# The 32x32 diagonal inverses of a chunked gated DeltaNet: a tile of their own, stored by transfers straight into block-diagonal tiles

## The chip, the cores and the metric

The kernel runs on one core of a Trainium2 chip. The metric is the device time of one execution in microseconds (us). All engines of the core run side by side, each through its own list of instructions in order: TensorE (PE, matmuls; PEld is its weight load), VectorE (DVE), ScalarE (ACT), GpSimd (POOL), and SyncE (SP), whose queue issues the transfers (DMAs).

## What is computed

The reference is a two-layer decoder step over 1024 prompt tokens and 8 x 4 sample tokens, model width 1024, in float32. Layer 0 is sliding-window attention, layer 1 a gated DeltaNet with 8 query/key heads and 16 value heads of width 128. The change touches only the chunked solve of layer 1's prompt part:

```python
lower = jnp.where(strict, jnp.einsum('nbhik,nbhjk->nbhij', kb, kc) * decay, 0.0)
rhs = jnp.concatenate([vc * bc[..., None], kb * jnp.exp(gc)[..., None]], axis=-1)
sol = lax.linalg.triangular_solve(lower + jnp.eye(chunk), rhs,
                                  left_side=True, lower=True, unit_diagonal=True)
...
def step(S, xs):
    u = w_v_c - jnp.einsum('bhck,bhkv->bhcv', w_k_c, S)
    o = jnp.einsum('bhck,bhkv->bhcv', q_dec_c, S) + jnp.einsum('bhij,bhjv->bhiv', qk_c, u)
    S = S * g_tot_c[..., None, None] + jnp.einsum('bhck,bhcv->bhkv', k_dec_c, u)
```

The kernel uses chunks of 128 tokens. It inverts each 128x128 unit triangular matrix: first its four 32x32 diagonal blocks, then the blocks beside them by matmuls.

## The kernel before

Layer 1 works on eight pairs r = 0 to 7, each one query/key head with its two value heads (`hq` in the code). A pair has 8 chunks times 2 heads = 16 triangular matrices, so 64 diagonal blocks. Beside this PE computes the large input projections of the layer (`ps_pj` in the profile; `project`, L548), 24 matmuls for each group of tokens. Each pair goes through these stages, each a Python generator that gives way wherever it says `yield`:

- `solve` (L1832): products k.kT on PE into PSUM, multiplied on DVE into the four tiles `UZ`; the diagonal 32x32 blocks go by 16 transfers to a DRAM tile `Ld`.
- `invert` (L1882): the 64 blocks come back as `X` (64 partitions, one block each, 32 x 32 in the free dimensions). POOL writes ones on the diagonal and zeros the diagonal blocks of `UZ`. Then DVE does 31 elimination steps of two instructions each (`tmp<-X`, `X<-X,tmp`). The block is stored as its transpose, so `X` holds the input above the diagonal and collects the inverse below it, in the same tile. `X` goes to DRAM (`Xdd`) and comes back as `Xc` (four transfers).
- `diagonal` (L1914), four times a pair: POOL multiplies `Xc` by a triangular mask, which drops the input still above the diagonal, into one of two block-diagonal tiles `Xd` (four instructions, 128 a kernel). PE multiplies `UZ` with `Xd`, ACT copies the product negated to `M`, DVE transposes `Xd`'s blocks into `UZ`.
- `blocks` (L1936): six rounds (v = 0 to 5) of small matmuls `ps_lg<-UZ,M`, each followed by DVE copies into `UZ`.
- `decayed` (L1961): products q.kT in two PSUM banks, 16 DVE instructions `DP<-ps_lg,sj,DP`, eight for each bank.
- `chain` (L1984): the recurrence over the 8 chunks. Each step starts with `ps_ob<-vo,UZ` on PE and goes PE, DVE, PE, DVE. It starts when round v = 2 of `blocks` is written.

**What sets the order of the work.** The program's order on each engine is fixed when the kernel is built. `Core` (L96) keeps modelled times of each engine. While PE's projections are written out one after another, `stages` (L496) goes through the list of waiting generators by rank and lets each run until a condition of its own fails, such as `idle("vector")` (the modelled DVE is free) or `soon(X)` (modelled data is nearly there). The ranks stand in the table `KR` (L242): for pair 1, `invert` has 10, `decayed` 35; for pair 0, `blocks` has 10. Two rules matter here. The PSUM banks `lg`, two of them, are handed out strictly in turn: `bank` (L535) waits until the bank used two requests ago was given back. And the projection of `kT` for pair r + 1 is not written out before chain r - 1 is finished (`until(lambda: finished[0] >= r - 1)`, L2171); so for r = 1 all projections stop until the chain of pair 0 is done.

The pool `gs` (opened at L1613 in `decays`, right side of SBUF) holds `X`, `tmp`, `Xc`, `Xd` and `M`; the pool `kwp` (L1319, left side) holds the split weights of the first `kT` projection until the end.

Of the kernel before, what the change touches and what calls it, by code (L numbers as in the profile page):

```python
# [5 lines left out]
F32 = mybir.dt.float32  # L6
# [3 lines left out]
ALU = mybir.AluOpType  # L10
# [4 lines left out]
P = 128  # L15
# [204 lines left out]
def body(tc, I, O, cst_ap, dbg=None):  # L220
    nc = tc.nc
    from contextlib import ExitStack, nullcontext
    es = ExitStack()
# [71 lines left out]
    C = {k: cst[:, o:o + w] for k, (o, w) in COFF.items() if o < nkeep}  # L295
# [189 lines left out]
    def weave(gen, name, hq=None):  # L485

        rank = KR[hq][name] if hq is not None else K[name]
        i = 0
        while i < len(jobs) and jobs[i][3] <= rank:
            i += 1  # L490
        jobs.insert(i, [lambda: True, gen, name, rank])
# [25 lines left out]
    def plain():  # L517
        return not isinstance(nc, Core)
# [4 lines left out]
    def soon(*ts):  # L523
        return lambda: plain() or nc.ready(ts) <= nc.free["tensor"] + AH
# [237 lines left out]
    if True:  # L762
# [469 lines left out]
        for t in range(NB + 1):  # L1232
            parts = P if t < NB else TS
            pv = psb("pj3")[0:parts, 0:256]
            n = 0
# [51 lines left out]
        nc = Core(tc)  # L1287
# [23 lines left out]
    if True:  # L1311
# [4 lines left out]
        hp = es.enter_context(tc.tile_pool(name="hp2", bufs=1, side="left"))  # L1316
        h2hi, h2lo = ([hp.tile([P, KD, b - a], F32R, tag=f"{nm}{i}", name=nm) for i, (a, b) in enumerate(GRP)]
                      for nm in ("h2hi", "h2lo"))
        kwp = es.enter_context(tc.tile_pool(name="kwp", bufs=1, side="left"))  # L1319
        x2_guard = tc.tile_pool(name="x2", bufs=1, side="left")  # L1320
        x2 = Watched(nc, x2_guard.__enter__(), since=nc.free["tensor"])
        nc.parts.add(x1d.tensor.name)
# [2 lines left out]
        kwr, kw = [], []  # L1325
# [110 lines left out]
        for i, t in enumerate(turned_):  # L1436
# [7 lines left out]
            for kk, hf in order if i < NB else sorted(order, key=lambda o: o[::-1]):  # L1444
                if True:
                    ns = slice(hf * 512, (hf + 1) * 512)
                    if hf not in pjs:
                        tag = ("pj", "pj", "mi", "mi")[outs[0] % 4]
# [50 lines left out]
    gs, Xd, gs_guard = None, [], None  # L1499

    def decays():
# [22 lines left out]
        for gi, (a, b) in enumerate(GRP):  # L1524
# [3 lines left out]
            n = 0  # L1528
# [81 lines left out]
        nc.vector.tensor_copy(gbs[:, 1, :], bt[:, :, NB])  # L1610
        ab2_guard.__exit__(None, None, None)
        ab_guard.__exit__(None, None, None)
        gs_guard = tc.tile_pool(name="gs", bufs=1, side="right")  # L1613
        gs = Watched(nc, gs_guard.__enter__(), since=nc.free["tensor"] + SL)
        for i in range(2):
            Xd.append(gs.tile([P, 4, P], F32, name=f"Xd{i}"))
            nc.gpsimd.memset(Xd[i], 0.0)
        weave(decay_blocks(0, states[0]), "decay")
        weave(solve(0, states[0]), "solve", 0)
        weave(decayed(0, states[0]), "decayed", 0)  # L1620
# [22 lines left out]
    if True:  # L1643
# [75 lines left out]
        def proj_kq(hq, st, which=(0, 1), run=None):  # L1719
            for nm, ct, s0 in [(("kT", HQ + hq, HQ), ("qT", hq, 0))[w] for w in which]:  # L1720
                full = gp.tile([P, T], F32, tag=nm, name=nm, bufs=2)
                st[nm] = full
                conv(ct, s0 + hq, lambda gi, a0, b0, full=full: full[:, a0:b0],
                     lambda gi, *a, nm=nm: st.update({nm + "done": gi == 2}), run)
            return st
# [81 lines left out]
        def spare(hq):  # L1807

            return "mi" if hq == 0 else "lg"
# [72 lines left out]
        def invert(hq, st, Ld, Xdd):  # L1882
            UZ, lg = st["UZ"], spare(hq)
            yield lambda: inverted[0] == hq


            X = gs.tile([64, 32, 32], F32, tag="X", name="X")
            tmp = gs.tile([64, 256], F32, tag="tmp", name="tmp")
            nc.sync.dma_start(X, Ld)
            yield soon(X)  # L1890
            nc.gpsimd.memset(X.rearrange("p i c -> p (i c)")[:, 0:1024:33], 1.0)
            for cp_ in range(4):
                uv = UZ[cp_].rearrange("p h c i -> p (h c) i")
                for b in range(4):
                    bs = slice(32 * b, 32 * b + 32)
                    nc.gpsimd.memset(uv[bs, :, bs], 0.0)
            yield soon(X)
            for k in range(31):
                n, m = 31 - k, k + 1
                tv = tmp[:, 0:n * m].rearrange("p (i c) -> p i c", c=m)  # L1900
                yield idle("vector")
                nc.vector.tensor_tensor(tv, X[:, k, k + 1:].unsqueeze(2).to_broadcast([64, n, m]),
                                        X[:, k, 0:m].unsqueeze(1).to_broadcast([64, n, m]), ALU.mult)
                nc.vector.tensor_tensor(X[:, k + 1:, 0:m], X[:, k + 1:, 0:m], tv, ALU.subtract)
            nc.sync.dma_start(Xdd, X)
            inverted[0] += 1
            yield lambda: solved[0] == hq
            Xc = gs.tile([P, 16, 32], F32, tag="Xc", name="Xc")
            for b in range(4):
                nc.sync.dma_start(Xc[32 * b:32 * b + 32], Xdd[16 * b:16 * b + 16].rearrange("q i c -> i q c"))  # L1910

            lg, Ms, uzs = "lg", [], [t_.rearrange("p h c i -> p (h c) i") for t_ in UZ]

            def diagonal():  # L1914

                for cp_, uz in enumerate(uzs):
                    xd = Xd[cp_ % 2]
                    yield soon(Xc)
                    for b in range(4):
                        bs = slice(32 * b, 32 * b + 32)  # L1920
                        nc.gpsimd.tensor_tensor(xd[bs, :, bs], Xc[bs, 4 * cp_:4 * cp_ + 4, :],
                                                C["lo32"][bs, :].unsqueeze(1).to_broadcast([32, 4, 32]), ALU.mult)
                    yield lambda: st.get("pairs", 0) >= cp_ - 2
                    yield ready(xd)
                    pm = yield from bank(lg)
                    pmv = pm.rearrange("p (q i) -> p q i", q=4)
                    for q in range(4):
                        nc.tensor.matmul(pmv[:, q, 0:96], uz[:, q, :], xd[:, q, 0:96], start=True, stop=True)
                    yield soon(pm)
                    M = gs.tile([P, 4, 96], F32, tag="M", name="M", bufs=3)  # L1930
                    nc.scalar.activation(M, pmv[:, :, 0:96], AF.Copy, scale=-1.0)
                    give(lg, pm)
                    nc.vector.transpose(uz.rearrange("p q i -> p (q i)"), xd.rearrange("p q i -> p (q i)"))
                    Ms.append(M)

            def blocks():  # L1936


                for v in range(6):
                    parts = [(v - s, 64 - 32 * s) for s in range(3) if 0 <= v - s < 4]  # L1940
                    yield lambda: len(Ms) > parts[0][0]
                    yield ready(*[Ms[cp_] for cp_, _ in parts], *[UZ[cp_] for cp_, _ in parts])
                    pz = yield from bank(lg)
                    pzv = pz.rearrange("p (q i) -> p q i", q=4)
                    for q in range(4):
                        for cp_, r0 in reversed(parts):
                            rs, cs = slice(r0, r0 + 32), slice(r0 + 32, P)
                            nc.tensor.matmul(pzv[rs, q, cs], Ms[cp_][:, q, rs], uzs[cp_][:, q, cs], start=True, stop=True,
                                             skip_group_check=True)
                    yield soon(pz)  # L1950
                    for cp_, r0 in reversed(parts):
                        rs, cs = slice(r0, r0 + 32), slice(r0 + 32, P)
                        nc.vector.tensor_copy(uzs[cp_][rs, :, cs], pzv[rs, :, cs])
                    give(lg, pz)
                    st["pairs"] = max(0, v - 1)
                solved[0] += 1

            weave(blocks(), "blocks", hq)
            weave(diagonal(), "blocks", hq)
# [194 lines left out]
        proj_kq(0, states[0], (0,), run_k)  # L2154
        w_raw(1)
        proj_kq(0, states[0], (1,), lambda evac: projected(evac, lambda: project(gin, None, P, h2hi, h2lo, evacs[0], kw, (2,))))
        for r in range(HQ):
            if r > 0:
                weave(chain(r - 1, states.pop(r - 1)), "chain", r - 1)
                weave(decayed(r, states[r]), "decayed", r)  # L2160
            if r > 0:
                proj_kq(r, states[r], (1,))
            if r + 1 < HQ:
                proj_z(2 * r)
                proj_z(2 * r + 1)
                states[r + 1] = {}
                weave(decay_blocks(r + 1, states[r + 1]), "decay")
                weave(solve(r + 1, states[r + 1]), "solve", r + 1)
                for what in "vk" if r in VK else "kv":
                    if what == "k":  # L2170
                        until(lambda: finished[0] >= r - 1)  # L2171
                        proj_kq(r + 1, states[r + 1], (0,))
                    else:
                        until(lambda: gs is not None and gated[0] >= 4 * (r - 1))
                        proj_v(r, states[r])
            else:
                proj_v(r, states[r])
                weave(chain(r, states.pop(r)), "chain", r)
                proj_z(2 * r)
                proj_z(2 * r + 1)  # L2180
# [499 lines left out]
    nc = nc.nc  # L2680
# [36 lines left out]
```

## Time and profile before

| | us |
|---|---|
| median of 3 runs (lowest, highest) | 1735.28 (1730.47, 1735.62) |
| the profiled execution, its own time | 1730.22 |
| its span | 1728.1 |
| PE busy in the span | 1628.6 |
| DVE busy | 1207.9 |
| ACT busy | 862.0 |
| POOL busy | 603.2 |

The profiled execution is one of the quicker ones: 5.06 us below the median. Of its 1730.22 us, 2.1 lie around the span. Nearly all instructions are recorded by a helper, so their line is L89; instructions are known by the names of the tiles that they write and read: `ps_lg<-Xd,UZ` is a product of `diagonal`, `tmp<-X` an elimination step, `ps_ob<-vo,UZ` a step of a chain. Rows of the timeline have start, duration, engine, line, operation, tiles, shapes and count; in brackets how long the engine had been idle and what ended that.

### The profile page before, as it was taken

The page shows a single profiled execution, that of the slowest core. Times are in us where ns is not written, and L with a number is a line of the kernel's source. Part 1 is how long each engine was busy: PE and PEld are TensorE (multiplying, and loading weights), DVE is VectorE, ACT ScalarE, POOL GpSimd, SP SyncE. Part 2 cuts the span into 40 slices and gives each one's busy share as a digit, 9 for nine tenths or more (in the row PEclk, how much of TensorE's full clock was granted, in tenths as well). Part 3 has the DMA queues.
Part 4 walks back from the last instruction along what each step waited for, and adds up shares of the span by engine and source line. Part 5 has one row for each costly group of instructions (what it writes and reads, how often), then busy time and mean ns, then how long its engine had stood idle before and what let it go on. Part 6 is the DMA issues. An engine that isn't in the chain of part 4 may idle for free. (4 is left out here: it accounts for less than half of the span.)

```text
span 1728.1 us, 31800 instructions
## 1 busy us (share of the span) xinstructions
PE 1628.6 (94%) x10666; PEld 1432.1 (83%) x10666; DVE 1207.9 (70%) x3538; ACT 862.0 (50%) x2514; POOL 603.2 (35%) x1170
## 2 busy tenths in 40 slices
PE   6999999998999899799999999999999998989897
PEld 5988888986777889689989999899998996667685
DVE  4526675564565678877887789778798876357677
ACT  4625555444334565256554665654756555332332
POOL 2601111112122334354443544545345454332322
PEclk9999999999999999899999999999999999999999
DMA  9542121233233232132412323224232137764785
GB/s 330 152 134 72 52 58 50 55 98 106 85 130 103 81 79 67 53 88 56 126 36 75 102 59 107 69 77 112 50 107 62 46 97 211 228 200 130 233 277 184
DMA packets 281573, 191.77 MB, mean 111 GB/s; under 512 B 98362, under 2 KB 253882, under 8 KB 281379
## 3 DMA queue, kind: packets, MB, share of 16 engines
q1 hardware_dynamic: 281410, 189.75, 38.1%
q8 instruction: 84, 1.38, 0.3%
q14 instruction: 79, 0.64, 0.1%
HBM read 144.68 MB, written 47.04 MB: 111 GB/s over the span
## 5 line engine op out<-in xcount | busy, mean ns | idle before, releaser
L89 PE MATMUL ps_pj<-h2hi,wl 128*128 128x384 f32 (+1 forms) x1128 | 380.4, 337 | 2.2 <-POOL wl L89 2.2
L89 PE MATMUL ps_pj<-h2hi,wh 128*128 128x384 f32 (+1 forms) x1128 | 378.3, 335 | 2.1 <-ACT wh L89 2.1
L89 PE MATMUL ps_pj<-h2lo,wh 128*128 128x384 f32 (+1 forms) x1128 | 379.4, 336 | 0.0
L89 POOL TENSOR_TENSOR wl<-wr,wh 128x512 fp32r<-128x512 f32 x122 | 164.4, 1348 | 517.5 <-ACT wh L89 432.9
L89 PEld LDWEIGHTS ps_pj<-h2hi,wl 128*128 128x128 f32 x1128 | 213.6, 189 | 6.2 <-POOL wl L89 3.1
L89 PEld LDWEIGHTS ps_pj<-h2hi,wh 128*128 128x128 f32 x1128 | 213.5, 189 | 4.3 <-ACT wh L89 2.4
L89 PEld LDWEIGHTS ps_pj<-h2lo,wh 128*128 128x128 f32 x1128 | 213.5, 189 | 3.2
L89 POOL TENSOR_TENSOR xt<-xt,y 128x512 f32<-128x512 f32 (+1 forms) x48 | 63.9, 1333 | 188.2 <-DVE y L89 165.1
L89 PE MATMUL ps_pj<-hlo,wh 128*128 128x384 f32 (+1 forms) x360 | 119.0, 331 | 0.0
L89 PE MATMUL ps_pj<-hhi,wh 128*128 128x384 f32 (+1 forms) x360 | 118.4, 329 | 0.0
L89 PE MATMUL ps_pj<-hhi,wl 128*128 128x384 f32 (+1 forms) x360 | 117.9, 328 | 0.0
L89 DVE SCALAR_TENSOR_TENSOR vT<-XR,cT,vT 128x384 f32<-128x384 f32 (+1 forms) x144 | 93.0, 658 | 29.0 <-ACT vT L89 27.1
L89 DVE TENSOR_TENSOR tmp<-X 64x31 f32<-64x31 f32 (+15 forms) x248 | 94.0, 379 | 10.4 <-POOL X L89 7.1
L89 DVE TENSOR_TENSOR X<-X,tmp 64x31 f32<-64x31 f32 (+15 forms) x248 | 94.6, 381 | 8.5
L89 ACT CAST wh<-wr 128x512 fp32r<-128x512 f32 x122 | 75.1, 616 | 16.4 <-PE ps_pj L89 12.0
L89 PEld LDWEIGHTS ps_pj<-hlo,wh 128*128 128x128 f32 x360 | 67.7, 188 | 11.2 <-issue 11.1
L89 ACT COPY XR<-ps_pj 128x384 f32<-128x384 f32 (+1 forms) x96 | 43.0, 448 | 55.9 <-PE ps_pj L89 55.7
L89 POOL TENSOR_TENSOR Xd<-Xc,cst 32x128 f32<-32x128 f32 x128 | 63.4, 495 | 21.2 <-DMA Xc<-Xdd 10.4
L89 PEld LDWEIGHTS ps_pj<-hhi,wh 128*128 128x128 f32 x360 | 67.7, 188 | 2.7 <-issue 2.7
L89 ACT ACTIVATE prob<-prob,nm 128x256 f32<-128x256 f32 (+1 forms) x128 | 62.2, 489 | 14.8 <-DVE nm L89 14.6
L89 PEld LDWEIGHTS ps_pj<-hhi,wl 128*128 128x128 f32 x360 | 67.7, 188 | 2.1 <-issue 2.1
L89 ACT ACTIVATE vo<-vo,fo 128x128 f32<-128x128 f32 x128 | 42.3, 392 | 54.0 <-POOL fo L89 54.0
(574 smaller groups left out, 4218.1 us busy)
## 6 DMA issues: line engine op xcount, KB each, us to landing
wr<-in_gdn_w_in SPq DMA_DIRECT2D x96, 256.0 KB
S<-in_state_gdn_s SPq DMA_DIRECT2D x40, 256.0 KB
xt<-in_x_prompt SPq DMA_DIRECT2D x16, 512.0 KB
wm<-in_w_mod SPq DMA_DIRECT2D x16, 512.0 KB
wr<-in_swa_w_in SPq DMA_DIRECT2D x64, 128.0 KB
wmod<-in_w_mod SPq DMA_DIRECT2D x32, 256.0 KB
wm<-in_w_mod SPq DMA_DIRECT2D x32, 256.0 KB
DP<-gcr SPq DMA_DIRECT2D x64, 128.0 KB
```

The lines of the kernel that those rows point to most:

```text
L89: inst = fn(*args, **kwargs)
```

## The change

`X` stays the input. The inverse is built in a second tile `Y` of the same shape, which POOL first sets to zero with ones on the diagonal. The elimination reads its multipliers from `X` and writes `Y`, so above `Y`'s diagonal there is nothing to mask. The four transfers from `Xdd` go straight to the diagonal blocks of one tile `Xd` for all 16 matrices, zeroed once; the tile `Xc`, the masks and their 128 POOL instructions are gone. `Y` and `Xd` need more room, so the pool `kwp` is closed after the projections that use it, and `gs` is opened only after that.

```diff
-        kwp = es.enter_context(tc.tile_pool(name="kwp", bufs=1, side="left"))
+        kwp_guard = tc.tile_pool(name="kwp", bufs=1, side="left")
+        kwp = kwp_guard.__enter__()
...
+        yield lambda: not kw
         gs_guard = tc.tile_pool(name="gs", bufs=1, side="right")
         gs = Watched(nc, gs_guard.__enter__(), since=nc.free["tensor"] + SL)
-        for i in range(2):
-            Xd.append(gs.tile([P, 4, P], F32, name=f"Xd{i}"))
-            nc.gpsimd.memset(Xd[i], 0.0)
+        Xd.append(gs.tile([P, 16, P], F32, name="Xd"))
+        nc.gpsimd.memset(Xd[0], 0.0)
...
             X = gs.tile([64, 32, 32], F32, tag="X", name="X")
+            Y = gs.tile([64, 32, 32], F32, tag="Y", name="Y")
             tmp = gs.tile([64, 256], F32, tag="tmp", name="tmp")
             nc.sync.dma_start(X, Ld)
-            yield soon(X)
-            nc.gpsimd.memset(X.rearrange("p i c -> p (i c)")[:, 0:1024:33], 1.0)
+            yv = Y.rearrange("p i c -> p (i c)")
+            yield lambda: plain() or nc.after(nc.used, Y, "gpsimd") <= nc.free["tensor"]
+            nc.gpsimd.memset(yv, 0.0)
+            nc.gpsimd.memset(yv[:, 0:1024:33], 1.0)
...
                 nc.vector.tensor_tensor(tv, X[:, k, k + 1:].unsqueeze(2).to_broadcast([64, n, m]),
-                                        X[:, k, 0:m].unsqueeze(1).to_broadcast([64, n, m]), ALU.mult)
-                nc.vector.tensor_tensor(X[:, k + 1:, 0:m], X[:, k + 1:, 0:m], tv, ALU.subtract)
-            nc.sync.dma_start(Xdd, X)
+                                        Y[:, k, 0:m].unsqueeze(1).to_broadcast([64, n, m]), ALU.mult)
+                nc.vector.tensor_tensor(Y[:, k + 1:, 0:m], Y[:, k + 1:, 0:m], tv, ALU.subtract)
+            nc.sync.dma_start(Xdd, Y)
             inverted[0] += 1
             yield lambda: solved[0] == hq
-            Xc = gs.tile([P, 16, 32], F32, tag="Xc", name="Xc")
             for b in range(4):
-                nc.sync.dma_start(Xc[32 * b:32 * b + 32], Xdd[16 * b:16 * b + 16].rearrange("q i c -> i q c"))
+                bs = slice(32 * b, 32 * b + 32)
+                nc.sync.dma_start(Xd[0][bs, :, bs], Xdd[16 * b:16 * b + 16].rearrange("q i c -> i q c"))
...
-                    xd = Xd[cp_ % 2]
-                    yield soon(Xc)
-                    for b in range(4):
-                        bs = slice(32 * b, 32 * b + 32)
-                        nc.gpsimd.tensor_tensor(xd[bs, :, bs], Xc[bs, 4 * cp_:4 * cp_ + 4, :],
-                                                C["lo32"][bs, :].unsqueeze(1).to_broadcast([32, 4, 32]), ALU.mult)
+                    xd = Xd[0][:, 4 * cp_:4 * cp_ + 4, :]
...
         proj_kq(0, states[0], (1,), ...)
+        kw.clear()
+        kwp_guard.__exit__(None, None, None)
```

Because `Xd` no longer waits for POOL in the model, and `X` can be loaded again while `Y` is being stored, the written order changes on every engine from the first diagonal product of pair 0 on; ahead of it PE's order is the same, the opening of `gs` included.

On DVE, at the start of pair 1's elimination (`DP` is `decayed` of pair 1, `UZ<-Xd` the transpose of pair 0's first diagonal block), the order before is:

```order
L89 TENSOR_SCALAR epq<-gsq 128x8
L89 SCALAR_TENSOR_TENSOR DP<-ps_lg,sj,DP 128x128 x16
L89 TENSOR_TENSOR tmp<-X 64x31
L89 TENSOR_TENSOR X<-X,tmp 64x31
L89 TENSOR_TENSOR tmp<-X 64x60
L89 TENSOR_TENSOR X<-X,tmp 64x30x2
L89 STREAM_TRANSPOSE UZ<-Xd_6530 128x512
```

and now, on DVE at the same place:

```order
L89 TENSOR_SCALAR epq<-gsq 128x8
L89 SCALAR_TENSOR_TENSOR DP<-ps_lg,sj,DP 128x128 x13
L89 TENSOR_TENSOR tmp<-X,Y 64x31
L89 TENSOR_TENSOR Y<-Y,tmp 64x31
L89 STREAM_TRANSPOSE UZ<-Xd 128x512
L89 TENSOR_TENSOR tmp<-X,Y 64x60
L89 TENSOR_TENSOR Y<-Y,tmp 64x30x2
```

The elimination starts three `DP` instructions earlier. From here to its end DVE has, now, the 60 remaining elimination instructions and nothing else; before, pair 0's other transposes, its `blocks` copies and most of chain 0's DVE instructions stood between them. Where the elimination ends, DVE now has:

```order
L89 TENSOR_TENSOR tmp<-X,Y 64x31
L89 TENSOR_TENSOR Y<-Y,tmp 64x31
L89 SCALAR_TENSOR_TENSOR DP<-ps_lg,sj,DP 128x128 x3
L89 STREAM_TRANSPOSE UZ<-Xd 128x512
L89 COPY UZ<-ps_lg 32x4x32
L89 COPY UZ<-ps_lg 32x4x64
L89 COPY UZ<-ps_lg 32x4x32
L89 STREAM_TRANSPOSE UZ<-Xd 128x512
L89 COPY UZ<-ps_lg 32x4x96
```

The last three `DP` instructions, which free one of the two `lg` banks, and all of pair 0's `blocks` copies have moved behind it. On PE, at the end of the projections that precede chain 0 (`ps_pj`; the four `32x32` are round v = 0 of pair 0), the order now is:

```order
L89 MATMUL ps_pj<-h2hi,wl 128x288
L89 MATMUL ps_lg<-Xd,UZ 128x96 x4
L89 MATMUL ps_lg<-UZ,M 32x32 x4
L89 MATMUL ps_lg<-UZ,M 32x64
L89 MATMUL ps_lg<-UZ,M 32x32
```

Before, on PE, the second diagonal product stood 15 projection matmuls ahead of that end, and round v = 0 another 25 ahead of it; now 8 projection matmuls stand ahead of the first diagonal product, 61 between it and the second, and none behind. The number of PE instructions is the same in all.

## Prediction

> **What bounds the kernel now.** I read first the page's busy times:
>
> ```profile
> span 1728.1 us, 31800 instructions
> PE 1628.6 (94%) x10666; PEld 1432.1 (83%) x10666; DVE 1207.9 (70%) x3538; ACT 862.0 (50%) x2514; POOL 603.2 (35%) x1170
> ```
>
> PE bounds the whole, POOL is far from it. So 128 POOL instructions taken away gain only where PE waits. Next the stretches (columns: length, busy time of PE, PEld, DVE, ACT, POOL, then PE's granted clock, DMA share, GB/s), cut where PE's projections stop and start again:
>
> ```profile
> 703.00:754.00 51.00, 38.40 (x281) 29.24 (x281) 42.10 (x126) 17.40 (x63) 15.96 (x55) 0.90 0.20 57
> 754.00:1440.00 686.00, 670.00 (x4729) 632.58 (x4729) 558.79 (x1521) 400.23 (x1253) 322.13 (x784) 1.00 0.30 81
> 1440.00:1728.00 288.00, 256.77 (x1246) 193.17 (x1244) 183.88 (x542) 97.92 (x238) 92.21 (x117) 0.95 0.70 212
> ```
>
> From 754 to 1440 PE idles 16.0 us of 686: nearly nothing to gain. The 51 us before are different. PE's timeline there:
>
> ```profile
> 701.07 1.02 PE L89 MATMUL ps_lg<-Xd,UZ 128*128 128x96 f32 x8
> ...
> 702.99 0.29 PE L89 MATMUL ps_pj<-h2hi,wl 128*128 128x288 f32 x1
> 705.24 1.23 PE L89 MATMUL ps_lg<-UZ,M 128*32 128x96 f32 x24 [1.96 <-DVE UZ L89]
> ...
> 708.22 1.08 PE L89 MATMUL ps_ob<-vo,UZ 128*128 128x128 f32 x4
> ...
> 714.96 0.71 PE L89 MATMUL ps_ob<-vo,UZ 128*128 128x128 f32 x4
> ...
> 733.13 0.75 PE L89 MATMUL ps_ob<-vo,UZ 128*128 128x128 f32 x4 [0.44 <-DVE vo L89]
> ...
> 737.40 0.74 PE L89 MATMUL ps_ob<-vo,UZ 128*128 128x128 f32 x4 [0.44 <-DVE vo L89]
> ...
> 744.04 0.71 PE L89 MATMUL ps_ob<-vo,UZ 128*128 128x128 f32 x4
> ...
> 754.11 0.42 PE L89 MATMUL ps_pj<-h2hi,wh 128*128 128x384 f32 x1
> ```
>
> The last projection is at 702.99, the next at 754.11. Between them PE has only chain 0 (first step 708.22) and small products; the projections of pair 2 may not start before that chain ends. Here the end is set by latency, and each microsecond by which chain 0 starts or ends later is one lost by PE. What DVE does in this stretch decides. Grouped from 692.05 to 732.25, pair 1's elimination is:
>
> ```profile
> L89 DVE TENSOR_TENSOR tmp<-X 64x31 f32<-64x31 f32 (+15 forms) x31 | 11.6, 374 | 2.3 <-POOL X L89 1.7
> L89 DVE TENSOR_TENSOR X<-X,tmp 64x31 f32<-64x31 f32 (+15 forms) x31 | 11.3, 363 | 1.1
> ...
> L89 DVE STREAM_TRANSPOSE UZ<-Xd 128x512 f32<-128x512 f32 x4 | 2.8, 704 | 0.0
> ```
>
> That is 11.6 + 11.3 = 22.9 us of work, interleaved before with pair 0's blocks and chain.
>
> **What the change removes.** POOL's masks, its wait for `X`, and the transfers they hang on:
>
> ```profile
> 683.11 0.51 SPq L89 DMA_DIRECT2D Xdd<-X  x1
> 686.09 1.95 SPq L89 DMA_DIRECT2D Xc<-Xdd  x4
> 688.08 0.50 SPq L89 DMA_DIRECT2D X<-Ld  x1
> ```
>
> ```profile
> 689.04 2.05 POOL L89 TENSOR_TENSOR Xd<-Xc,cst 32x128 f32<-32x128 f32 x4
> 691.87 0.16 POOL L89 MEMSET X<- 64x32 f32 x1 [0.79 <-DMA X<-Ld]
> 691.93 3.71 POOL L89 MEMSET UZ<- 32x128 f32 x16
> ```
>
> Four masks take 2.05 us between transfer and first product; without them pair 0's first product could come that much earlier. The added zeroing of `Y` covers 64 x 1024. POOL's nearest row, two 128x512 fills of `Xd`, is 0.99 us, so I estimate about 1 us for each pair, 8 us in all, against 128 masks that go:
>
> ```profile
> L89 POOL TENSOR_TENSOR Xd<-Xc,cst 32x128 f32<-32x128 f32 x128 | 63.4, 495 | 21.2 <-DMA Xc<-Xdd 10.4
> ```
>
> ```profile
> 591.13 0.99 POOL L89 MEMSET Xd<- 128x512 f32 x2 [2.31 <-DVE gbs L89]
> ```
>
> POOL's balance is -55 us, hidden either way behind PE. The one-tile `Xd` is zeroed at the same place as the two were. Pair 0's own elimination keeps its order and time.
>
> **What the new order does at chain 0.** In SP's queue pair 1's `X` load now stands ahead of pair 0's `Xdd`: 0.5 us of issue (row at 688.08), so `Xdd` goes at about 683.6 and the `Xd` transfers at about 686.6 to 688.5. How long they take to land is seen at pair 2:
>
> ```profile
> 859.35 2.05 SPq L89 DMA_DIRECT2D Xc<-Xdd  x4
> ...
> 862.63 0.87 POOL L89 TENSOR_TENSOR Xd<-Xc,cst 32x128 f32<-32x128 f32 x1 [1.81 <-DMA Xc<-Xdd]
> 864.55 3.57 POOL L89 TENSOR_TENSOR Xd<-Xc,cst 32x128 f32<-32x128 f32 x7 [1.05 <-DMA Xc<-Xdd]
> ```
>
> The first lands 3.3 us after its issue. Both old and new transfers are cut into rows of 32 floats on the DRAM side, so I keep 3.3: the last lands at 691.8, the first product ends at 692.8, DVE's transpose (0.70) at 693.5. The early start thus gains nothing here: SP's order and the wait for four transfers eat the 2 us.
>
> From there DVE must run 60 elimination instructions before anything of pair 0. Their first two, and the `DP` instructions, are on DVE's timeline:
>
> ```profile
> 688.22 1.90 DVE L89 SCALAR_TENSOR_TENSOR DP<-ps_lg,sj,DP 128x128 f32<-128x128 f32 x7 [0.72 <-PE ps_lg L89]
> ...
> 692.06 0.18 DVE L89 TENSOR_TENSOR tmp<-X 64x31 f32<-64x31 f32 x1 [1.68 <-POOL X L89]
> 692.28 0.21 DVE L89 TENSOR_TENSOR X<-X,tmp 64x31 f32<-64x31 f32 x1
> ```
>
> The elimination's 22.9 us, less 0.4 for these two, plus the idle between its instructions (2.3 - 1.7 + 1.1 = 1.7), are 24.2, so it ends at 717.7. Then come three `DP` of 0.27 each (1.90 / 7), 0.8 in all: 718.5. Only then is the `lg` bank of round v = 0 free, and DVE free to copy. PE runs out of projections at about 703 as before and idles some 15 us. From the third diagonal product to chain 0's start took 708.22 - 701.07 = 7.15 us before, with rounds 1 and 2 inside. The same must follow now, with v = 0 and without elimination steps between; I take 7.1. **Chain 0 starts at 725.6, 17.4 us later than 708.22.**
>
> Some of it comes back, since the elimination is out of the chain's way. A step without other work took 737.40 - 733.13 = 4.27 us; with diagonal products and transposes of pair 1 inside, 744.04 - 737.40 = 6.64; the first, with rounds 3 to 5 of pair 0, 714.96 - 708.22 = 6.74. Now all of pair 1's products and rounds stand in steps 1 and 2. I take 6.74 + 2 x 6.64 + 5 x 4.27 = 41.4, plus 0.5 for the last step's output: 41.9, against 754.11 - 708.22 = 45.9 before. Projections restart at 725.6 + 41.9 = 767.5, 13.4 later. And what pair 1 needed of PE after 754 is now done in the idle time; grouped from 752 to 766:
>
> ```profile
> L89 PE MATMUL ps_lg<-UZ,M 128*32 128x96 f32 (+2 forms) x48 | 2.5, 233 | 0.0
> ```
>
> So 13.4 - 2.5 = **10.9 us lost** here. The change also adds a wait: with one `Xd`, pair 1's four transfers may not start before pair 0's last transpose, near chain 0's start at 725.6. Issued over 1.95 us and landed 3.3 later, they are there at about 731, just ahead of step 1 (725.6 + 6.74 = 732.3), in front of which PE needs them; behind them on SP stand transfers of pair 2's `DP` rows and pair 0's outputs, not needed before the chain's end. I take 0. The bounds of this term: if the elimination runs 1.5 us faster without masks on POOL beside it, and every step takes 4.27 (34.7 in all), it is 10.9 - 1.5 - 7.2 = 2.2; if all steps take 6.2, their mean from 708.22 to 733.13, it is 50.1 - 41.9 = 8.2 more, 19.1.
>
> The later pairs: PE's waits from 754 to 1440 for the masks are
>
> ```profile
> PE ps_lg L89 <- POOL Xd L89: 4.2, 3, 1.9
> PE ps_mi L89 <- DVE S L89: 2.5, 2, 2.1
> PE ps_mi L89 <- ACT uo L89: 1.9, 3, 1.0
> PE ps_tr L89 <- ACT vT L89: 1.8, 2, 1.3
> PE ps_pj L89 <- POOL wl L89: 1.5, 1, 1.5
> ```
>
> 4.2 us in three places (first row). The masks go, but the model now places the products earlier, and the transfers still take, at pair 2, from 859.35 to 864.55. So the wait may go (-4.2) or change into one for the transfers; the row at 864.55 shows 1.05 of it, and at six pairs of up to 1.9 (the longest above) less the 4.2 paid it would cost 7 more. I take 0, between them. The POOL zeroing of `UZ`, written before the weights' low halves, may hold back a projection by up to its 3.71 us at pair 1, inside the idle time; elsewhere PE waits 1.5 us for `wl` in all (last row), and I take 0. The end from 1440 keeps its order with shifts of some 20 matmuls: 0, give or take 2.
>
> Sum: 1730.22 + 10.9 = 1741.1 for an execution like the profiled one. The median before lies 5.06 above it, so the forecast is 1735.28 + 10.9, rounded **1746**.
>
> **One rule of the Trainium skill.** The clock first, in stretches before, around a gap of 3.25 us:
>
> ```profile
> 580.00:584.00 4.00, 1.69 (x10) 1.37 (x8) 3.76 (x10) 1.61 (x5) 2.09 (x4) 1.00 0.26 67
> ...
> 588.00:592.00 4.00, 4.00 (x22) 3.83 (x22) 1.82 (x6) 2.17 (x7) 1.60 (x5) 0.79 0.21 69
> ```
>
> ```profile
> 584.93 0.71 PE L89 MATMUL ps_lg<-gpr,cst 128*128 128x128 f32 x4 [3.25 <-DVE gpr L89]
> ```
>
> After the gap the granted clock is 0.79. The Trainium skill, TensorE: Matmul & The Clock Gate, "Part 1: The HAM clock gate", says that an idle window of about 3.4 us halves the clock until about 3.4 us were busy; by that rule a 15 us hole leaves the chain a cold PE, and this trace agrees as far as the row goes.
>
> **The rivals.** *A cold chain* (slow side): the hole lowers the clock for chain 0, whose sparse steps don't raise it again. For it: 0.79 above and 0.90 in the stall. Against: the steps at 733 to 754 came after sparse ones, too, and took 4.27. Its price is the step of 6.2: +19.1, 1754.
>
> *The elimination pays for itself* (ends not slower): pair 1's elimination must run once anyway; done in one piece, it leaves chain 0 at 4.27 a step, pair 1's products fit into DVE's waits, and the masks' waits are gone as well: +2.2 - 4.2 = -2, 1733. It decides if block work adds under about 1 us to a step; the 6.64 step speaks against it.
>
> *Given back later*: in the new order pair 1's solve is over early, and the chains of later pairs stand some 20 matmuls further ahead, so waits like those for `S`, `uo` and `vT` above may go as well as the masks'. All five rows make 11.9; if 7 of them go, it is +3.9, 1739. Against it: each comes from a chain that runs beside PE's work, and new places make new waits. That the change doesn't take effect at all, because `gs` would open later, the order excludes.
>
> **How the numbers follow.** A measurement of this kernel tells about 0.3% (5.2 us) from no change. Chances: forecast 0.62, cold chain 0.14, pays for itself 0.14 (half of it faster by over 0.3%, with gains at the end too), given back 0.10. The slow cases make 0.76 less 0.02 of the forecast's low edge: slower 0.74, same 0.19, faster 0.07. The range takes in the bounds 2.2 - 4.2 and 19.1 plus part of the 7: 1733 to 1758.
>
> **What would show it.** Right: the last projection before chain 0 still near 703, a PE hole of some 15 us behind it, put down to DVE `UZ` or `DP`; pair 1's `tmp<-X,Y` in one unbroken run of about 24 us; chain 0's first `ps_ob` near 725, projections again near 767; no `Xd` on POOL, and POOL about 55 us less busy. Wrong: a chain start before 715; steps of chain 0 near 6 us; PE waits on `Xd` transfers of over 10 us later; or a gain from 754 to 1440 greater than PE's 16 us of idle time there leave room for.

## The result and the profile after

The changed kernel takes 1782.92 us (median of 4 runs, 1780.39 to 1784.01), the kernel before beside it 1735.45 (4 runs): ratio 1.0272, 95% interval 1.0251 to 1.0293. It is 47.5 us slower, where 10.9 were forecast; the direction was right, the size was not, and 1782.9 lies above the forecast's range of 1733 to 1758. The profiled execution took 1780.39 us.

The page of the changed kernel, with POOL relieved by 603.2 - 548.3 = 54.9 us and PE busy for 20.9 us longer, with the same 10666 instructions:

```profile
span 1778.6 us, 31613 instructions
## 1 busy us (share of the span) xinstructions
PE 1649.5 (93%) x10666; PEld 1449.0 (81%) x10666; DVE 1200.1 (67%) x3538; ACT 862.6 (48%) x2514; POOL 548.3 (31%) x1049
```

The two spans lie 50.5 us apart. PE idles 29.6 us of them longer; for the other 20.9 the same instructions keep it busy, at a mean granted clock of 0.968 instead of 0.983 over the span.

The three stretches of the prediction, cut at the last projection before chain 0, the first after it and the start of chain 7; columns as there. (The cut at 1440 of before lies 4.5 us behind the start of its chain 7, 1435.53.)

```profile
704.00:772.00 68.00, 44.85 (x375) 34.04 (x373) 49.70 (x138) 18.23 (x64) 8.62 (x37) 0.84 0.16 44
772.00:1475.00 703.00, 666.88 (x4574) 628.25 (x4574) 534.93 (x1502) 393.44 (x1239) 272.85 (x690) 0.98 0.28 75
1475.00:1778.00 303.00, 272.13 (x1353) 206.80 (x1352) 193.46 (x554) 104.72 (x252) 98.36 (x121) 0.95 0.69 209
```

The first is 17 us longer than the 51 of before, as the prediction had it in kind. The second is the surprise: 36 us idle in 703, where before it was 16 in 686, and the granted clock 0.98 instead of 1.00. And chain 7, at which it ends, stands 58 projection matmuls earlier in PE's row (the order of its instructions) than before, so the last stretch holds more work.

PE's timeline at chain 0 in the changed kernel:

```profile
704.67 0.29 PE L89 MATMUL ps_pj<-h2hi,wl 128*128 128x288 f32 x1
704.80 1.03 PE L89 MATMUL ps_lg<-Xd,UZ 128*128 128x96 f32 x8
706.41 0.44 PE L89 MATMUL ps_lg<-UZ,M 128*32 128x32 f32 x8 [0.58 <-ACT M L89]
722.04 1.06 PE L89 MATMUL ps_lg<-UZ,M 128*32 128x64 f32 x16 [15.19 <-DVE UZ L89]
723.03 2.02 PE L89 MATMUL ps_lg<-Xd,UZ 128*128 128x96 f32 x8
...
728.88 0.92 PE L89 MATMUL ps_ob<-vo,UZ 128*128 128x128 f32 x4
...
772.28 0.67 PE L89 MATMUL ps_pj<-h2hi,wh 128*128 128x384 f32 x1
```

The hole is there, 15.19 us long, ended by DVE's `UZ`. DVE's timeline shows what stood in front of it, pair 1's elimination in one piece from 695.98 to 720.2, then the three `DP`, and only then pair 0:

```profile
695.98 0.17 DVE L89 TENSOR_TENSOR tmp<-X,Y 64x60 f32<-64x60 f32 x1
...
720.09 0.18 DVE L89 TENSOR_TENSOR Y<-Y,tmp 64x31 f32<-64x31 f32 x1
720.20 0.85 DVE L89 SCALAR_TENSOR_TENSOR DP<-ps_lg,sj,DP 128x128 f32<-128x128 f32 x3
720.98 0.70 DVE L89 STREAM_TRANSPOSE UZ<-Xd 128x512 f32<-128x512 f32 x1
```

What PE waited for from 772 to 1475 (columns: in all, times, longest):

```profile
PE ps_tr L89 <- ACT vT L89: 12.8, 11, 2.1
PE ps_lg L89 <- DMA Xd<-Xdd: 8.7, 4, 3.6
PE ps_mi L89 <- DVE us L89: 4.6, 3, 2.4
PE ps_tr L89 <- ACT XR L89: 3.0, 3, 1.9
```

The first row was 1.8 us in two places before: transposes of v that stand in PE's row ahead of what ACT has delivered. The second takes the place of the masks' 4.2.

### The profile page after: what moved, and what is told of

Read it like the earlier page. It is cut to its first block, busy times and chain, and to the rows that moved or that the text cites. A ratio compares the mean times of both kernels' runs of the same rounds, so it can differ in the third digit from the quotient of the medians.

```text
span 1778.6 us, 31613 instructions
## 1 busy us (share of the span) xinstructions
PE 1649.5 (93%) x10666; PEld 1449.0 (81%) x10666; DVE 1200.1 (67%) x3538; ACT 862.6 (48%) x2514; POOL 548.3 (31%) x1049
## 5 line engine op out<-in xcount | busy, mean ns | idle before, releaser
L89 PE MATMUL ps_pj<-h2hi,wh 128*128 128x384 f32 (+1 forms) x1128 | 383.2, 340 | 2.1 <-ACT wh L89 2.1
L89 DVE SCALAR_TENSOR_TENSOR vT<-XR,cT,vT 128x384 f32<-128x384 f32 (+1 forms) x144 | 89.4, 629 | 54.2 <-ACT vT L89 52.2
L89 DVE TENSOR_TENSOR tmp<-X,Y 64x31 f32<-64x31 f32 (+15 forms) x248 | 89.7, 362 | 13.2 <-DMA X<-Ld 9.7
L89 DVE TENSOR_TENSOR Y<-Y,tmp 64x31 f32<-64x31 f32 (+15 forms) x248 | 90.5, 365 | 8.5
L89 POOL TENSOR_TENSOR rst<-rsw 128x4 f32<-128x4 f32 x96 | 24.2, 252 | 163.8 <-DVE rsw L89 127.4
```

The lines of the kernel that those rows point to most:

```text
L89: inst = fn(*args, **kwargs)
```

## Experiments 1: the operations or the order

The planner (`Core`, L96) books each instruction's modelled time when it is written out. So an instruction can be issued without being booked (`hide`), and one can be booked that isn't issued (`issued` with no instruction). This separates what the change does on the chip from the order that it brings. Theory A: the loss is the order. Theory B: it is the operations. `Told` makes a stand-in for a tile that exists for the planner alone. The edit of e1, at two places of several, without the lines `if told:` and `else:` that choose between the two ways:

```diff
-                nc.sync.dma_start(Xd[0][bs, :, bs], xq)
+                nc.hide("sync", "dma_start", Xd[0][bs, :, bs], xq)
+                nc.issued("sync", "dma_start", None, (Told(tXc, 32, 16, 32), xq), {})
...
+                    yield soon(Told(tXc))
+                    for b in range(4):
+                        nc.issued("gpsimd", "tensor_tensor", None, (tXd, Told(tXc), C["lo32"]), {})
```

The second part books the four masks, which no longer exist. In the traces, e1 has DVE's and ACT's order of before, row for row, and PE's too but for the order among small `ps_lg<-UZ,M` that stand side by side. In e2 the roles are exchanged: masks and `Xc` are issued, the costs of the change are booked. e3 and e4 book the former costs for some pairs only (`told = hq < 2` and `told = hq >= 2`).

> All operations of the change (inverse in Y, transfers straight into one Xd, no masks), but the planner is told the former costs, so PE, DVE and ACT have the order of the kernel before, row for row. Theory A (the loss is the order alone): the time of before, 1735, or up to 8 us less, since the masks' waits of 4.2 us go; no PE hole near 705. Theory B (the loss is in the operations: one Xd shared by all pairs, the transfers' landing, the zeroing on POOL): near 1783 in the old order, too.

Measured: 1727.5 us (12 runs; before beside it 1734.8), ratio 0.9959, 0.9942 to 0.9976. All operations of the change in the old order are a gain of 7 us.

> The counterpart: all operations of the kernel before (X in place, Xc, 128 masks, two Xd), but the planner is told the costs of the change, so PE and ACT have the order of the changed kernel. Theory A: 1783 or more, up to 1800, since every first diagonal product also waits for four masks (2 us a pair). Theory B: near 1735.

Measured: 1821.7, ratio 1.0501 (1.0470 to 1.0531). That is above the 1800 that theory A allowed. The old operations in the new order are 39 us worse than the new ones in it; PE waits 22.9 us for the masked `Xd` from 780 to 1505. So the operations gain in either order, and the order loses with either set of operations. Theory B fell.

> The changed kernel; the planner is told the former costs for pairs 0 and 1 only, so chain 0 stands as before (pair 1's elimination spread through it), and from pair 2 on the order is the changed kernel's. If the hole ahead of chain 0 makes the whole loss (cold clock and later waits follow from it): 1735 to 1740. If loss is split as the traces have it (18 us at the restart of the projections, some 30 later by itself): 1783 - 18 = 1765.

Measured: 1765.6, ratio 1.0176 (1.0151 to 1.0202). The loss is split; the hole does not make all of it.

> The changed kernel; the planner is told the former costs for pairs 2 to 7 only, so chain 0 stands behind pair 1's elimination as in the changed kernel, and later chains stand where they stood before. If the hole makes the whole loss: 1783. If the loss is split: 1735 + 18 = 1753, with the PE hole of 15 us near 706 still there.

Measured: 1743.3, ratio 1.0053 (1.0033 to 1.0072), with the hole of 15.24 us still in its trace. It lies 10 us below the 1753 of its forecast, which counted from 1735; from e1's 1727.5 it is 15.8 more.

Together, in medians:

| step | us |
|---|---|
| operations alone: e1 against before | -7.3 |
| order at chain 0: e4 against e1 (the changed kernel against e3: 17.3) | +15.8 |
| order of pairs 2 to 7: e3 against e1 (the changed kernel against e4: 39.6) | +38.0 |
| sum | +46.5 |
| the changed kernel against before | +47.5 |

The windows of e1, e3 and e4 from the restart of the projections to chain 7, one fence for each kernel:

```profile
762.00:1437.00 675.00, 663.57 (x4684) 628.05 (x4682) 540.47 (x1513) 399.28 (x1249) 279.18 (x692) 1.00 0.31 81
```

```profile
763.00:1458.00 695.00, 661.41 (x4623) 622.33 (x4623) 539.44 (x1509) 392.10 (x1239) 272.38 (x690) 0.99 0.28 76
```

```profile
771.00:1448.00 677.00, 664.81 (x4632) 627.68 (x4630) 536.65 (x1506) 397.75 (x1248) 278.09 (x692) 0.99 0.30 81
```

PE idles 11.4 us in e1, 12.2 in e4, and 33.6 in e3, the only one of the three with the new order of the later pairs. Idle time is not all: e3's span is 33.7 us longer than e1's (1765.3 against 1731.6), and PE is busy for 12.6 us of it (1641.9 against 1629.3), with the same number of instructions.

## Experiments 2: which wait carries the 38 us

e3's waits in that stretch:

```profile
PE ps_tr L89 <- ACT vT L89: 15.5, 13, 2.3
PE ps_lg L89 <- DMA Xd<-Xdd: 7.0, 4, 3.6
```

Theory V: the first row carries the loss. Theory X: the second does. Three kernels take them apart by postponing the waiting instruction in PE's row (e5 with the first hunk, e6 with the second, e7 with both). The fourth, e8, asks whether any new plan loses (theory T), with the first hunk and 2 us in e1.

```diff
-                        yield ready(u, st["irk"])
+                        late = 3.0 if hq >= 2 else 0.0
+                        yield lambda: plain() or nc.ready((u, st["irk"])) + late <= nc.free["tensor"]
...
-                    yield ready(tXd if told else xd)
+                    late = 0.0 if told else 2.0
+                    yield lambda: plain() or nc.ready((tXd if told else xd,)) + late <= nc.free["tensor"]
```

> As e3_early_as_before (1765.6, with PE waits of 15.5 us for ACT vT in 13 places and 7.0 us for the Xd transfers in 4), but the planner puts the transposes of v of pairs 2 to 7 into PE's row 3 us later than it holds them ready; diagonal products and transfers keep their places within some 40 matmuls. Theory V (those transposes stand ahead of what ACT and DVE really deliver; the waits and the clock behind them are the loss): the vT waits fall below 4 us, time 1745 to 1753. Theory X (the diagonal products that wait for the direct transfers carry the loss): 1760 or more, with the vT waits gone but others in their place.

Measured: 1754.5 (ratio 1.0105, 1.0074 to 1.0135), 11 us less than e3. The vT waits are gone, and the first row of its list of waits from 752 to 1437 is now

```profile
PE ps_lg L89 <- DMA Xd<-Xdd: 6.7, 6, 2.5
```

The time just misses theory V's 1745 to 1753, and 27 of the 38 us remain: the waits for vT were at most part of the loss.

> As e3_early_as_before, but the planner puts the diagonal products of pairs 2 to 7 into PE's row 2 us later than it holds Xd landed. Theory V: the Xd waits go, the vT waits stay near 15, time 1757 to 1762 (7 us of waits at most). Theory X: the loss goes with these waits, 1740 or less.

Measured: 1768.7 (1.0190, 1.0159 to 1.0220): no gain, and above theory V's 1757 to 1762 as well. Its Xd waits fell to 3.0 us, but vT stayed at 13.0 and waits of transposes for ACT's `vo` came up with 7.0. Theory X fell.

> Both postponements together (v transposes 3 us, diagonal products 2 us, pairs 2 to 7). If the two kinds of wait are the loss: 1735 to 1745, both waits below 4 us. If any new plan loses against the table of ranks whatever it waits for (theory T: the ranks fit one plan only): 1755 or more.

Measured: 1753.1 (1.0102, 1.0076 to 1.0128), between the two forecasts. The vT waits are zero, those for Xd 4.6 us; new ones came up, `vo` with 9.0 in ten places. Waits that are postponed one by one come back elsewhere.

> The order of before with the operations of the change (e1_order_of_before, 1727.5), and only the transposes of v of pairs 2 to 7 planned 2 us later; the rest is planned anew around them. Theory T (every new plan loses): 1740 or more. Theory V (a plan loses only by waits that PE really meets): within 6 us of 1727.5.

Measured: 1731.6 (0.9985, 0.9966 to 1.0003), 4 us above e1. So it is not so that every new plan loses; theory T fell.

Then the plan itself was read. Where no projection may be written out, `until` (L507) lets the modelled PE pass 0.1 us and runs the waiting generators. Counted after 500 us of the planner's time, the kernel before runs dry for 38.4 us, the changed one for 71.9. Chain 0's condition (`finished`, L2171) grew from 24.9 to 36.2. And the wait for the next weights to be split (ACT writes `wh`, POOL `wl`; L563 and L593) grew from 1.8 to 24.5 us (some 21 in e3, 6.6 in e4). The split waits for a modelled idle ACT; in the new order it rarely finds one in time. While projections are missing, the planner writes out transposes of v and products right behind each other. (The postponements of before moved the weights, too: their wait is 13.6 us in e5's plan and 17.6 in e7's, so these two do not measure the transposes alone.) Theory W: this is the cause of the vT waits on the chip. The edit, in effect from the end of chain 0:

```diff
-                        yield idle("scalar", raws[i + 1][q])
+                        yield ready(raws[i + 1][q]) if eager else idle("scalar", raws[i + 1][q])
```

> As e3_early_as_before (1765.6), but from the end of chain 0 on the planner splits the next weights as soon as they are loaded and their turn has come, and no longer waits until it holds ACT idle for it. In the plan the time in which the projections have no split weights falls from 21.5 us to 0.5 us (before: 1.8). Theory W (in the new order the plan finds ACT busy when the next weights are due, runs out of projections, and puts v transposes and products straight one behind the other, where PE then really waits): 1732 to 1742, vT waits below 4 us. If the weights' place is not the cause: 1755 or more.

Measured: 1749.3 (1.0093, 1.0070 to 1.0117), 16 us less than e3. From 758 to 1465:

```profile
PE ps_lg L89 <- DMA Xd<-Xdd: 7.1, 3, 3.9
PE ps_tr L89 <- ACT vT L89: 3.7, 5, 1.4
```

The vT waits went from 15.5 to 3.7 us though nothing was edited at those transposes, and PE's busy time is 1631.1 us, near e1's 1629.3 again, not e3's 1641.9. The edit also made the whole plan anew, so other instructions moved with the weights. The time is 7 us above the upper end of theory W's forecast.

> The changed kernel itself, with the weights split in the same way (and ahead of other waiting work); nothing of the former costs is told. The plan's time without weights falls from 24.5 us to 0.1; its hole ahead of chain 0 stays. Theory W: as with the late pairs in the old order (1743.3), 1740 to 1750. Otherwise 1770 or more.

Measured: 1761.7 (1.0162, 1.0128 to 1.0195): 21 us less than the changed kernel and 12 above theory W's forecast, between its two cases; its Xd waits are 10.1 us in three places. In e10, and in e12 to e14, the generator that splits the weights also gets the first rank (`K["ahead"] = -1`) from the end of chain 0 on.

> Control: the kernel before, with the weights split in the same way. Its plan had weights in time (1.8 us without them, now 1.5), so theory W gives no gain: 1730 to 1745. If the early split were a gain of its own for any order: 1715 or less.

Measured: 1742.9 (1.0059, 1.0036 to 1.0082). In the old order the same edit costs about 9 us (before beside it 1733.8). So the weights' place is worth between 16 us (e3 to e9 as measured) and 25 us (if the edit has its cost of 9 there too) of the 38.

## Experiments 3: another table, and the transfers' queue

Two kernels keep every operation of the change, the eager split of e10, and no former cost; only the table `KR` (L242) is another, chosen so that the plan runs dry for little time. Of e12's table, the row of pair 1:

```diff
-    KR = [... {'chain': 0, 'output': 3, 'solve': 12, 'invert': 10, 'blocks': 35, 'decayed': 35}, ...]
+    KR = [... {'chain': 10, 'output': 0, 'solve': 12, 'invert': 0, 'blocks': 8, 'decayed': 5}, ...]
```

> The changed kernel with the weights split eagerly as in e10_after_weights_eager, and another table of ranks, chosen so that the plan itself lets PE run dry as little as possible: after 500 of the plan's us, 16.2 us in all (71.9 in the changed kernel, 38.4 before), none of them for chain 0, which starts some 190 projection matmuls earlier, beside projections. Theory W (the change's loss is a plan that runs dry, under a table that fits the former costs): no hole behind 700, time 1705 to 1730. If a plan's dryness tells nothing about the chip: 1745 or more.

Measured: 1735.0 (12 runs; before 1734.7), ratio 1.0000, 0.9984 to 1.0015. Table and eager split together take back the whole 47.5 us, though not the 7 more of e1; the forecast's upper end was 1730. Its longest stretch without projections is now 645 to 671, where the changed kernel has 68 us, and chain 0 no longer lies in it: it starts at 689.69, beside projections.

```profile
645.00:672.00 27.00, 11.27 (x84) 9.81 (x84) 22.69 (x61) 9.80 (x23) 1.55 (x5) 0.66 0.15 30
```

```profile
656.78 5.41 PE L89 MATMUL ps_lg<-Xd,UZ 128*128 128x96 f32 x24 [11.43 <-DVE vT L89]
```

The plan has no stop for chain 0, but on the chip PE stands still for 11.43 us here, in front of pair 0's first diagonal products: pair 0's elimination ends at 650.7, and its `Xd` transfers are issued from 653.68 to 655.60.

> As e12_table_searched with a second table, found from another start: the plan runs dry for 31.7 us in all, 21.2 of them in front of pair 2's projections (24.9 before), none for weights. Theory W: 1722 to 1740. If the plan tells nothing: 1745 or more.

Measured: 1756.1 (1.0120, 1.0093 to 1.0147), 16 us above theory W's range. A plan that runs dry for less than that of before (31.7 us against 38.4) loses 21 us. From 752 to 1455 PE waits

```profile
PE ps_lg L89 <- DMA Xd<-Xdd: 17.3, 5, 6.6
PE ps_tr L89 <- ACT vT L89: 10.5, 4, 5.1
```

which the plan does not contain; in e12 the wait for `Xd` is 3.7 us from 672 to 1431. Why the transfers are late was read in the changed kernel, at its longest wait. SP's queue, then PE:

```profile
1320.73 0.51 SPq L89 DMA_DIRECT2D Xdd<-Y  x1
1325.69 0.38 SPq L89 DMA_DIRECT2D wr<-in_gdn_w_in  x1
1326.12 0.50 SPq L89 DMA_DIRECT2D zd<-th  x1
1326.71 2.12 SPq L89 DMA_DIRECT2D Xd<-Xdd  x4
```

```profile
1330.95 3.70 PE L89 MATMUL ps_lg<-Xd,UZ 128*128 128x96 f32 x16 [3.65 <-DMA Xd<-Xdd]
```

Between `Xdd` and `Xd` stands a load of weights, for whose buffer SP waits 4.4 us on POOL's `wl`. Theory Q: the queue makes the transfers late. The last two kernels let POOL issue them, with the orders of PE, DVE and ACT unchanged (the first of the two edited places):

```diff
-            nc.sync.dma_start(Xdd, Y)
+            nc.nc.gpsimd.dma_start(Xdd, Y)
+            nc.issued("sync", "dma_start", None, (Xdd, Y), {})
```

> As e13_table_searched_b (1756.1, PE waits of 17.3 us for the Xd transfers in 5 places), the rows of PE, DVE and ACT unchanged; only the transfers Xdd<-Y and Xd<-Xdd are issued by POOL instead of standing in SP's queue. Theory Q (the transfers come late because they stand in SP's queue behind loads of weights that wait for POOL's wl): the Xd waits fall below 8 us, time 1742 to 1750. If the two hops themselves take that long: waits and time as before, 1753 or more; more still if POOL, which waits at these transfers, now holds up wl.

Measured: 1815.6 (1.0461, 1.0428 to 1.0495), 59.5 us more than e13; the waits for `Xd` rose from 17.3 to 51.0 us.

> The changed kernel (1782.9, Xd waits of 8.7 us in 4 places from 772 to 1475), rows of PE, DVE and ACT unchanged, the same transfers issued by POOL. Theory Q: at most 6 us less, 1776 to 1780, and the vT waits of 12.8 us stay; so SP's queue is the small part of the changed kernel's loss. Otherwise 1783 or more.

Measured: 1841.5 (1.0606, 1.0580 to 1.0633), 59 us more than the changed kernel. PE's waits for the transfers rose from 8.7 to

```profile
PE ps_lg L89 <- DMA Xd<-Xdd: 49.2, 6, 9.2
```

because POOL issues four transfers far more slowly than SP, as its timeline at pair 2 shows:

```profile
881.57 0.60 POOL L1909 DMA_DIRECT2D Xdd<-Y  x1 [2.35 <-DVE Y L89]
885.39 0.72 POOL L1916 DMA_DIRECT2D Xd<-Xdd  x1 [3.22 <-DMA Xdd<-Y]
889.61 0.66 POOL L1916 DMA_DIRECT2D Xd<-Xdd  x1 [3.50 <-issue]
892.42 0.65 POOL L1916 DMA_DIRECT2D Xd<-Xdd  x1 [2.16 <-issue]
894.88 0.66 POOL L1916 DMA_DIRECT2D Xd<-Xdd  x1 [1.80 <-issue]
```

So theory Q is not decided: both kernels brought a cost larger than the one they were to take away. What e15 shows is that 40.5 us more wait for `Xd` came with 59 us more time in this order. That POOL was late with `wl` instead is not the reason: PE waits 2.3 us for it in e15, 2.0 in the changed kernel.

## Why the prediction was wrong, point by point

- **The hole: right.** Last projection 704.67 (703 forecast), hole 15.19 us (some 15) ended by DVE's `UZ`, the elimination in one piece for 24.3 us (about 24), POOL 54.9 us less busy (55).
- **Chain 0's start and end: right in kind, too small.** It starts at 728.88, not 725.6, and projections come back at 772.28, not 767.5, 4.8 us later than forecast. Of these, 2.5 lie ahead of DVE's piece, which began at 695.98, not 693.5: pair 0's `Xdd` was issued at 687.28, where 683.6 was reckoned. Some 0.8 lie behind the hole, where eight products took 2.02 us at 723.03 and again at 727.06; in the 7.15 us that the forecast was made from, only one of the two eights was that slow (row below). The last 1.5 lie in the chain, 43.4 us instead of 41.9. Against 10.9 forecast, e4 against e1 measures 15.8. The 1.5 us that the lower bound took off the elimination came from no row: it took 12.3 + 10.3 = 22.6 us, where 22.9 were reckoned.

```profile
701.07 1.02 PE L89 MATMUL ps_lg<-Xd,UZ 128*128 128x96 f32 x8
706.40 2.02 PE L89 MATMUL ps_lg<-Xd,UZ 128*128 128x96 f32 x8
```

- **The cold chain** (rival): it fell. The granted clock was at 1.00 again from 730 to 770. The first three steps took 6.7 to 7.3 us with pair 1's work inside; from 749.72 on they took 4.0 to 5.1, near the 4.27 of before. The hole made only what stands ahead of the chain, and its first products, cold.
- **The masks: mis-sized.** Their waits of 4.2 us go and e1 measures a gain of 7.3, where 0 was taken.
- **"I take 0, between them", for the later pairs, and "0, give or take 2" for the end: the step that failed.** e3 against e1 measures +38.0. The bounds -4.2 and +7 were made for the transfers' wait alone, and that size was right (8.7 us against 4.2). But the step took "some 20 matmuls further ahead" for a shift that keeps the neighbours together and priced new waits for the transfers and for `wl` alone; `vT` stands in it only among the waits that may go. What changed was who stands between whom: in the planner's order, projections are missing where the next weights are not split, and v's transposes stand there with no projections beside them to fill PE's time until ACT has delivered. The runs show the weights' share, 16 us as measured and up to 25 if e11's cost is counted, and that a new table with the eager split takes all 47.5 back.
- **"Nearly nothing to gain"** from 754 to 1440 was right for gains; it says nothing on losses. A stretch in which PE idles 16 us in 686 has little to gain by a new order and, as the 36 us idle in it now show, something to lose.
- **Open:** the rest of the 38, some 13 to 22 us. Late transfers behind SP's queue are seen in rows, but not proved by a run; how much is theirs was not settled, nor why `Xd` is late by 17.3 us in e13's order and by 3.7 in e12's. Transfers issued by ACT were not tried.

The fastest version measured is e1: the change's operations in the order of before, 1727.5 us, 0.4% ahead of the kernel before.

## What to carry to other kernels

Where a planner writes the order, a change of operations is two changes; issue it once with the old costs booked, and the two come apart in one run. Here the operations gained 7 us and the order lost 55 (the changed kernel against e1). A table of ranks fitted to old costs has to be fitted again before the change is judged; where the plan runs dry is a good first place to look, but here it foresaw neither the late transfers of e13 nor the 11.43 us of e12.

## What the runs showed of the hardware

The granted clock in the changed kernel, in windows of 1 us around the hole (PE's last work before it ends at 706.85, the first after it starts at 722.04):

```profile
708.00:709.00 1.00, 0.00 (x0) 0.00 (x0) 0.93 (x3) 0.00 (x0) 0.00 (x0) 1.00 0.47 132
709.00:710.00 1.00, 0.00 (x0) 0.00 (x0) 0.93 (x3) 0.00 (x0) 0.00 (x0) 0.50 0.02 1
...
728.00:729.00 1.00, 1.00 (x7) 1.00 (x6) 0.48 (x2) 0.00 (x0) 0.00 (x0) 0.50 0.00 0
729.00:730.00 1.00, 1.00 (x15) 0.87 (x17) 0.84 (x2) 0.49 (x1) 0.00 (x0) 0.76 0.00 0
730.00:731.00 1.00, 1.00 (x24) 0.66 (x20) 0.83 (x3) 0.37 (x1) 0.00 (x0) 1.00 0.14 23
```

It fell to 0.50 some 2 us after PE fell idle and came back about 7 us after work began, with one gap of 0.44 us in between. The Trainium skill, TensorE: Matmul & The Clock Gate, "Part 1: The HAM clock gate", gives about 3.4 us of sustained work, in windows that run freely, before the clock is full again; this trace agrees with windows of that length, if the first of the two, with the gap in it, did not count as busy.

A hole is not needed for a low clock. At the end of chain 0, where PE's gaps are at most 0.70 us from 749.72 on, the changed kernel shows

```profile
770.00:772.00 2.00, 2.00 (x8) 1.52 (x7) 1.02 (x3) 0.65 (x3) 0.00 (x0) 0.61 0.22 66
772.00:774.00 2.00, 2.00 (x9) 2.00 (x9) 0.42 (x1) 1.01 (x5) 0.00 (x0) 0.54 0.04 11
```

and the kernel before is at 0.50 from 706 to 708, 724 to 726 and 730 to 732. What set these off no run shows.

A transfer takes longer to issue on POOL: four of 64 KB took 9.5 us from the first issue to the last at pair 2 of e15 and 7.8 at pair 1, against 1.9 to 2.4 for all four on SP in the changed kernel (2.12 in the row at 1326.71). The Trainium skill, DMA: Bandwidth & Descriptors, "Issuing engine by pattern", gives plain loads and stores to SyncE; the trace agrees.
